# A table of places for the wide halves of a two-layer decoder: the first pair's row block pairs at other distances, its sweep in fewer steps

## The chip, the cores and the metric

The kernel runs on one core of a Trainium2 chip. The time is that of one execution on the device in microseconds (us); the median of three runs of the kernel before is 2098.84 us, the lowest 2098.13 and the highest 2099.01. The engines have short names in the profile: PE is TensorE (PEld its weight loads), DVE is VectorE, ACT is ScalarE, POOL is GpSimd, and SPq is the queue of SyncE, which here issues nearly all DMAs.

## The reference

The kernel computes a trunk of two decoder layers over 256 tokens of width 2048, all in fp32. Layer 0 mixes tokens by attention with a forget gate, layer 1 by a mixture of dilated windows; behind each mixer comes an MLP, and the change lies in the two MLPs alone:

```python
def sq_relu_mlp(h, w_up, w_down):
    a = jax.nn.relu(h @ w_up)
    return (a * a) @ w_down

def reference(x, ...):
    for i in range(DEPTH):
...
        x = x + mix.astype(x.dtype)
        h = rms_norm(x, mlp_norm_g[i])
        x = x + sq_relu_mlp(h, mlp_w_up[i], mlp_w_down[i]).astype(x.dtype)
    return x
```

`w_up` is 2048 x 8192 and `w_down` is 8192 x 2048, so that the weights of one MLP fill 128 MB and each is read once.

## The kernel before

**Products.** Every weight matrix is read in row block pairs: a tile `raw` holds two blocks of 128 rows by 512 columns. ScalarE rounds it to `wh` (fp32r, line L403), VectorE makes the remainder `wl` = raw - wh (L404), and TensorE multiplies the transposed activations by both. Such a triple raw, wh, wl is called a piece here. A plain piece takes 12 matmuls of 128x512 (L452 to L454: two row blocks, two tiles of 128 tokens, three products hi*hi, hi*lo and lo*hi). An output of 512 columns takes 8 plain pieces, and the kernel counts them: a count is one plain piece. Pieces are prepared five ahead of TensorE (`W_BUFS`), and `raw` tiles are loaded five ahead of those (`RAW_BUFS`).

**Wide halves.** Of the 16 outputs of `h @ w_up` in an MLP (4 blocks b of 4 outputs n) ten are made two at a time by a Strassen-Winograd scheme, with seven products where the plain way takes eight. Its two by two are two token tiles and two row blocks on one side, two row blocks and two outputs on the other. One row block pair of such a pair of outputs is a triple of pieces, 6 matmuls each (L1119 to L1121): the "crossed" piece (two `raw` tiles are read for it, `raw` n-1 and n), the "differences" piece, whose source `sd` VectorE makes at L400, and the "sums" piece, whose source `v` VectorE makes at L406 and L407. They go into PSUM tiles named wide_n_tp, wide_n_sc and wide_n_acc. A row block pair costs VectorE three L404, one L400, one L406 and one L407. The last product of the seven is plain row blocks again; one piece of 6 matmuls serves two row block pairs, and these four pieces at a pair's end are called its sweep. Behind a pair's last triple `wide_chain` combines the six PSUM tiles on VectorE (L1083 to L1090), squares on ScalarE, transposes on VectorE (L1037) and sends the result through device memory: sixteen DMAs of 64 KB write it (`held`, L359), four read it back later (`back`).

**Token sums.** The activation side of the scheme needs sums and differences of the transposed activations of each of the 8 row block pairs. `token_sums` makes them during the first pair: four operations on VectorE (L568 to L573, tile `room`), a rounding on ScalarE (L587) and a remainder on VectorE (L591). Its waits are counted in steps of the jobs, and a step is one row block of a plain piece or one piece of a triple.

**What sets the order.** The program is recorded in one order and pinned to it; no scheduler moves anything. `Jobs` runs the side jobs (token sums, chains of finished products) at steps. `wide_slots` says behind which count a piece of a triple stands, and it is read twice: by `add_mlp`, which puts the loads and the preparation into the plan, and by `mlp`, which puts the matmuls there. There are five pairs, in `WIDE`: (1, 0) comes first and is the one that runs beside the token sums; counts 0 to 15 are the first two outputs, 16 to 31 the other two of block 0, 32 to 39 and 40 to 47 the first two outputs of the product with `w_down`.

SyncE's queue issues DMAs strictly in the program's order, each waits on one of eight semaphores that the DMA eight before it used, and a `raw` load waits until its buffer has been read.

Of the kernel before, what the change touches and what calls it, by code (L numbers as in the profile page):

```python
# [23 lines left out]
KC = D // P  # L24
# [22 lines left out]
SUM_TAGS = ("kh3", "kl3", "kh4", "kl4", "kh5", "kl5", "q0", "q1", "q2", "qkw0", "qkw1", "qkw2", "pT", "t1")  # L47

WIDE = ((1, 0), (2, 0), (2, 2), (3, 0), (3, 2))
WIDE_FROM = 15  # L50
UP_ALONE = ((2, 3), (2, 3), (), ())


def wide_slots():

    count = WIDE_FROM
    for b, n in WIDE:
        for pr in range(KC // 2):
            while count % 8 not in (7, 2, 5):
                count += 1  # L60
            yield count, (b, n, 0, pr)
            yield count, (b, n, 1, pr)
            yield count + 1, (b, n, 2, pr)
            count += 2
        count += count % 8 != 7
        for pr in range(0, KC // 2, 2):
            yield count, (b, n, 3, pr)
            count += count % 8 != 7 or pr % 4 == 2
        count += 1


class Jobs:
# [52 lines left out]
def trunk(ctx: ExitStack, tc, x, fox_w_in, fox_b_f, fox_q_gain, fox_k_gain, fox_w_out, dil_w_in,  # L125
# [202 lines left out]
    def add_mlp(l):  # L328
        woven["count"] = 0
        for at, (b, n, what, pr) in wide_slots():  # L330
            woven["due"].setdefault(at, []).append((mlp_w_up[l], b * D + n * NC, what, pr))
        for b in range(4):
            if b == 0:
                add_group(*((mlp_w_up[l], [(n * NC, NC)]) for n in range(2)))
            for n in UP_ALONE[b]:
                add(mlp_w_up[l], (0, D), [(b * D + n * NC, NC)])
            down = mlp_w_down[l][b * D:(b + 1) * D]
            together = 3 if b == 3 else 0
            add_group(*((down, [(n * NC, NC)]) for n in range(together)), parts=LAST_DOWN_PARTS)
            for n in range(together, NX):  # L340
                add(down, (0, D), [(n * NC, NC)])
        woven["due"] = {}
# [785 lines left out]
    def mlp(tag, **after):  # L1128
# [21 lines left out]
        for at, slot in wide_slots():  # L1150
            woven["due"].setdefault(at, []).append(slot)
# [149 lines left out]
```

## Time and profile before

| what | value |
|---|---|
| median of three runs | 2098.84 us |
| the profiled execution's own time | 2096.45 us |
| its span in the profile | 2094.6 us |
| TensorE busy | 2080.3 us, 9835 matmuls |
| VectorE busy | 1730.1 us |
| ScalarE busy | 1294.0 us |
| mean granted TensorE clock | 0.998 |
| loads of 512 KB from `w_up`, issue to landing | median 5.0 us |
| writes of 64 KB (`held`), first MLP and second MLP | median 4.5 and 4.3 us |

Times below are us from the start of the span. In the profile a row of the timeline gives start, duration, engine, line, operation and operands; a number in brackets is the engine's idle time before it, with what ended it. A matmul's record lasts longer than its share, since matmuls overlap: the distance of two starts is what it costs. The tiles' buffer numbers are left out in the profile (`wl`), and stand in the listings of the order (`wl162`, the remainder of piece 162). The first pair of the first MLP begins with piece 144, that of the second MLP with piece 620.

### The profile page before, as it was taken

The numbers are of one execution on the slowest core, as the hardware profiler recorded it, in microseconds if no ns is written. First come the engines' busy times: TensorE is split into PE (matmuls) and PEld (weight loads), VectorE is DVE, ScalarE is ACT, GpSimd is POOL, SyncE is SP. The second block draws the span as 40 slices with busy tenths as digits, with TensorE's granted clock in tenths as the row PEclk, the third lists the DMA queues.
The fourth block names the chain that finished last, engine by engine and source line by source line (L and its number), as shares of the span: only waits on it lengthen the run. The fifth ranks groups of instructions, "written<-read, shape, count | busy, mean of one in ns | idle before, by whom it ended". The sixth has DMA issues, their size and how long they took to land.

```text
span 2094.6 us, 28771 instructions
## 1 busy us (share of the span) xinstructions
PE 2080.3 (99%) x9835; PEld 1825.0 (87%) x9835; DVE 1730.1 (83%) x2215; ACT 1294.0 (62%) x1777; POOL 134.8 (6%) x142
## 2 busy tenths in 40 slices
PE   9999999999999999999999999999999999999999
PEld 7888888878888888888888888888888888888888
DVE  6888876998889889888668787767998899898874
ACT  6565654766666757574656565556666676666662
POOL 2000000000010011010010010000000100110100
PEclk9999999999999999999999999999999999999999
DMA  8888877878898898898877876868878988988985
GB/s 259 253 266 258 261 248 222 256 255 263 272 279 269 266 287 261 275 281 252 282 245 229 249 237 210 264 209 243 265 245 271 277 278 259 275 275 274 276 278 169
DMA packets 385874, 539.02 MB, mean 257 GB/s; under 512 B 43752, under 2 KB 177216, under 8 KB 385728
## 3 DMA queue, kind: packets, MB, share of 16 engines
q1 hardware_dynamic: 371488, 524.21, 78.9%
q0 software_dynamic: 13824, 12.59, 4.0%
q8 instruction: 77, 1.26, 0.3%
q10 hardware_dynamic: 416, 0.39, 0.1%
q14 instruction: 69, 0.57, 0.1%
HBM read 484.09 MB, written 40.39 MB: 250 GB/s over the span
## 4 chain that ended last, share of the span: by engine, by line
PE 87%; DVE 6%; DMA 3%; issue 1%; ACT 1%; SPq 1%; POOL 0%; DVEq 0%; ACTq 0%; POOLq 0%
PE acc L452 23%; PE acc L453 23%; PE acc L454 23%; DVE wl L404 3%; PE wide_n_tp L1120 2%; PE wide_n_tp L1119 2%; PE wide_n_tp L1121 2%; DMA raw<-in_mlp_w_up_dram 2%; PE wide_n_sc L1120 2%; PE wide_n_sc L1121 2%; PE wide_n_sc L1119 1%; PE wide_n_acc L1121 1%; PE wide_n_acc L1119 1%; PE wide_n_acc L1120 1%; ACT wh L403 1%
## 5 line engine op out<-in xcount | busy, mean ns | idle before, releaser
L404 DVE TENSOR_TENSOR wl<-raw,wh 128x1024 fp32r<-128x1024 f32 (+1 forms) x763 | 919.8, 1214 | 305.8 <-ACT wh L403 292.1
L403 ACT CAST wh<-raw 128x1024 fp32r<-128x1024 f32 (+1 forms) x763 | 787.7, 1045 | 531.0 <-PE acc L454 350.3
L452 PE MATMUL acc<-wh,hT_n 128*128 128x512 f32 x1280 | 487.7, 381 | 0.3 <-ACT hT_n L610 0.3
L453 PE MATMUL acc<-wl,hT_n 128*128 128x512 f32 x1280 | 486.8, 380 | 0.3 <-DVE wl L404 0.3
L454 PE MATMUL acc<-wh,hT_n 128*128 128x512 f32 x1280 | 486.3, 380 | 0.0
L454 PEld LDWEIGHTS acc<-wh,hT_n 128*128 128x128 f32 x1280 | 243.0, 190 | 34.2 <-DVE hT_n L611 0.4
L453 PEld LDWEIGHTS acc<-wl,hT_n 128*128 128x128 f32 x1280 | 243.2, 190 | 33.7 <-DVE wl L404 1.6
L452 PEld LDWEIGHTS acc<-wh,hT_n 128*128 128x128 f32 x1280 | 243.2, 190 | 33.0 <-ACT hT_n L610 0.6
L454 PE MATMUL acc<-wh,aTl_n1a 128*128 128x512 f32 x512 | 194.4, 380 | 0.0
L452 PE MATMUL acc<-wh,aTh_n1a 128*128 128x512 f32 x512 | 194.3, 380 | 0.0
L453 PE MATMUL acc<-wl,aTh_n1a 128*128 128x512 f32 x512 | 194.3, 380 | 0.0
L454 PE MATMUL acc<-wh,aTl_n3a 128*128 128x512 f32 x480 | 182.3, 380 | 0.0
L453 PE MATMUL acc<-wl,aTh_n3a 128*128 128x512 f32 x480 | 182.2, 380 | 0.0
L452 PE MATMUL acc<-wh,aTh_n3a 128*128 128x512 f32 x480 | 182.1, 379 | 0.0
L975 POOL DMA_DIRECT2D x<-y_n x96 | 84.2, 1364 | 970.8 <-ACT y_n L974 914.8
L403 ACT CAST wh<-sd 128x1024 fp32r<-128x1024 f32 x80 | 84.0, 1050 | 85.8 <-DVE sd L400 64.4
L403 ACT CAST wh<-v 128x1024 fp32r<-128x1024 f32 x80 | 84.0, 1050 | 50.6 <-PE acc L454 38.9
L454 PEld LDWEIGHTS acc<-wh,aTl_n1a 128*128 128x128 f32 x512 | 97.0, 189 | 13.7 <-DVE aTl_n1a L1069 0.2
L452 PEld LDWEIGHTS acc<-wh,aTh_n1a 128*128 128x128 f32 x512 | 97.0, 190 | 13.4
L453 PEld LDWEIGHTS acc<-wl,aTh_n1a 128*128 128x128 f32 x512 | 97.0, 190 | 13.5
L400 DVE TENSOR_TENSOR sd<-raw,raw 128x1024 f32<-128x1024 f32 x80 | 97.6, 1220 | 8.3 <-DMA raw<-in_mlp_w_up_dram 8.1
L454 PEld LDWEIGHTS acc<-wh,aTl_n3a 128*128 128x128 f32 x480 | 91.0, 190 | 12.8 <-DVE aTl_n3a L1069 0.2
(659 smaller groups left out, 3093.3 us busy)
## 6 DMA issues: line engine op xcount, KB each, us to landing
raw<-in_mlp_w_up_dram SPq DMA_DIRECT2D x296, 512.0 KB, 5.0
raw<-in_mlp_w_down_dram SPq DMA_DIRECT2D x256, 512.0 KB, 5.2
raw<-in_dil_w_in_dram SPq DMA_DIRECT2D x192, 256.0 KB, 3.9
raw<-in_fox_w_in_dram SPq DMA_DIRECT2D x94, 512.0 KB, 5.0
raw<-in_fox_w_out_dram SPq DMA_DIRECT2D x32, 512.0 KB, 4.7
raw<-in_dil_w_in_dram SPq DMA_DIRECT2D x32, 512.0 KB, 5.9
raw<-in_dil_w_out_dram SPq DMA_DIRECT2D x32, 512.0 KB, 4.5
x<-y_n POOLq DMA_DIRECT2D x96, 128.0 KB, 6.4
```

What stands on the lines that cost most here:

```text
L400: nc.vector.tensor_sub(quarters[0], raw, raws[n - 1][:, 1, :].unsqueeze(1).to_broadcast([P, RAW_SUB, NC]))
L403: nc.scalar.copy(hi[:, part, :], raw[:, part, :])
L404: nc.vector.tensor_sub(lo[:, part, :], raw[:, part, :], hi[:, part, :].bitcast(F32))
L452: nc.tensor.matmul(acc[t], ah[:, tok], hi, start=first, stop=False)
L453: nc.tensor.matmul(acc[t], ah[:, tok], lo, start=False, stop=False)
L454: nc.tensor.matmul(acc[t], al[:, tok], hi, start=False, stop=last)
L975: nc.gpsimd.dma_start(xt[n][:, t, h * HC:h * HC + HC], y, accum_op=ALU.add)
L1119: nc.tensor.matmul(banks[bank], ah, wh, start=what < 3 and of == 0, stop=False, **alone)
L1120: nc.tensor.matmul(banks[bank], ah, wl, start=False, stop=False, **alone)
L1121: nc.tensor.matmul(banks[bank], al, wh, start=False, stop=of == KC // 2 - 1, **alone)
```

## The change

The function that computed the places by a rule becomes a table of numbers, one row for each pair: eight places for its row block pairs, then four for its sweep. For four of the five pairs the table holds the numbers that the rule gave. For the first pair they differ: its row block pairs stood behind counts 15, 18, 21, 23, 26, 29, 31, 34 and now stand behind 15, 19, 23, 26, 29, 31, 34, 37; its sweep stood behind 37, 38, 39, 39 and now stands behind 39, 39, 40, 40. The second pair begins behind count 42 in both. The table is used in both MLPs. No instruction is added or removed; lines below the table have numbers five lower.

```diff
--- before.py
+++ after.py
@@ -47,26 +47,21 @@
 SUM_TAGS = ("kh3", "kl3", "kh4", "kl4", "kh5", "kl5", "q0", "q1", "q2", "qkw0", "qkw1", "qkw2", "pT", "t1")
 
 WIDE = ((1, 0), (2, 0), (2, 2), (3, 0), (3, 2))
-WIDE_FROM = 15
+WIDE_AT = ((15, 19, 23, 26, 29, 31, 34, 37, 39, 39, 40, 40), (42, 45, 47, 50, 53, 55, 58, 61, 63, 63, 64, 65),
+           (69, 71, 74, 77, 79, 82, 85, 87, 90, 91, 92, 93), (95, 98, 101, 103, 106, 109, 111, 114, 117, 118, 119, 119),
+           (122, 125, 127, 130, 133, 135, 138, 141, 143, 143, 144, 145))
 UP_ALONE = ((2, 3), (2, 3), (), ())
 
 
 def wide_slots():
 
-    count = WIDE_FROM
-    for b, n in WIDE:
+    for (b, n), at in zip(WIDE, WIDE_AT):
         for pr in range(KC // 2):
-            while count % 8 not in (7, 2, 5):
-                count += 1
-            yield count, (b, n, 0, pr)
-            yield count, (b, n, 1, pr)
-            yield count + 1, (b, n, 2, pr)
-            count += 2
-        count += count % 8 != 7
+            yield at[pr], (b, n, 0, pr)
+            yield at[pr], (b, n, 1, pr)
+            yield at[pr] + 1, (b, n, 2, pr)
         for pr in range(0, KC // 2, 2):
-            yield count, (b, n, 3, pr)
-            count += count % 8 != 7 or pr % 4 == 2
-        count += 1
+            yield at[KC // 2 + pr // 2], (b, n, 3, pr)
 
 
 class Jobs:
```

VectorE in the first MLP, around the first pair's fourth row block pair: twelve rows before the change, up to the "differences" piece of that row block pair (`wl162<-sd`).

```order
L404 TENSOR_TENSOR wl160_4466<-raw157_4355,wh160_4465 128x1024
L1066 TENSOR_TENSOR aTl_n1a0_1_4457<-back_n1a0_1_0_4357,aTh_n1a0_1_4456 128x4x128
L400 TENSOR_TENSOR sd_159_4481<-raw159_4388,raw158_4369 128x1024
L404 TENSOR_TENSOR wl161_4480<-raw159_4388,wh161_4479 128x1024
L406 TENSOR_TENSOR v_159_4482<-raw159_4388,sd_159_4481 128x512
L407 TENSOR_TENSOR v_159_4482<-raw158_4369,v_159_4482 128x512
L568 TENSOR_TENSOR room_n1_3806<-hT_n1_6_4012 128x512
L571 TENSOR_TENSOR room_n1_3806<-room_n1_3806 128x128
L572 TENSOR_TENSOR room_n1_3806<-room_n1_3806 128x128
L573 TENSOR_TENSOR room_n1_3806<-room_n1_3806 128x256
L1069 TENSOR_TENSOR aTl_n1a0_1_4457<-back_n1a0_1_1_4371,aTh_n1a0_1_4456 128x4x128
L404 TENSOR_TENSOR wl162_4504<-sd_159_4481,wh162_4503 128x1024
```

VectorE now, at the same number of pieces:

```order
L399 TENSOR_TENSOR wl159_4449<-sd_157_4430,wh159_4448 128x1024
L1061 TENSOR_TENSOR aTl_n1a0_1_4453<-back_n1a0_1_0_4357,aTh_n1a0_1_4452 128x4x128
L399 TENSOR_TENSOR wl160_4470<-raw158_4377,wh160_4469 128x1024
L1064 TENSOR_TENSOR aTl_n1a0_1_4453<-back_n1a0_1_1_4365,aTh_n1a0_1_4452 128x4x128
L399 TENSOR_TENSOR wl161_4489<-v_157_4431,wh161_4488 128x1024
L563 TENSOR_TENSOR room_n1_3806<-hT_n1_6_4012 128x512
L566 TENSOR_TENSOR room_n1_3806<-room_n1_3806 128x128
L567 TENSOR_TENSOR room_n1_3806<-room_n1_3806 128x128
L568 TENSOR_TENSOR room_n1_3806<-room_n1_3806 128x256
L399 TENSOR_TENSOR wl162_4513<-raw159_4392,wh162_4512 128x1024
L399 TENSOR_TENSOR wl163_4528<-raw160_4410,wh163_4527 128x1024
L586 TENSOR_TENSOR sums_n1_6_1_4519<-room_n1_3806,sums_n1_6_0_4518 128x512
```

Piece 162 belonged to the fourth row block pair; it is a plain piece now, and the fourth row block pair (`sd_162`) begins only behind piece 163; the remainders of the transposed activations (`aTl`) and the token sums (`room`) stand at nearly the same pieces as they did.

SyncE's queue at the second pair's first two row block pairs (`raw191/192` and `raw196/197` serve the first and second, `raw200/201` the third): before.

```order
L359 DMA held_n1a1_1_0_5109<-turned_n1a1_1_0_5108 32x4x128 x4
L378 DMA raw194_5140<-in_mlp_w_down_dram 128x2x512
L359 DMA held_n1a1_1_1_5124<-turned_n1a1_1_1_5123 32x4x128 x4
L378 DMA raw195_5174<-in_mlp_w_down_dram 128x2x512
L378 DMA raw196_5191<-in_mlp_w_up_dram 128x2x512
L378 DMA raw197_5193<-in_mlp_w_up_dram 128x2x512
L378 DMA raw198_5229<-in_mlp_w_down_dram 128x2x512
L359 DMA held_n1a1_0_0_5232<-turned_n1a1_0_0_5231 32x4x128 x4
L359 DMA held_n1a1_0_1_5241<-turned_n1a1_0_1_5240 32x4x128 x4
L378 DMA raw199_5277<-in_mlp_w_down_dram 128x2x512
L378 DMA raw200_5293<-in_mlp_w_up_dram 128x2x512
L378 DMA raw201_5310<-in_mlp_w_up_dram 128x2x512
```

And now:

```order
L373 DMA raw194_5144<-in_mlp_w_down_dram 128x2x512
L373 DMA raw195_5156<-in_mlp_w_down_dram 128x2x512
L373 DMA raw196_5185<-in_mlp_w_up_dram 128x2x512
L373 DMA raw197_5187<-in_mlp_w_up_dram 128x2x512
L354 DMA held_n1a1_1_0_5190<-turned_n1a1_1_0_5189 32x4x128 x4
L373 DMA raw198_5221<-in_mlp_w_down_dram 128x2x512
L354 DMA held_n1a1_1_1_5203<-turned_n1a1_1_1_5202 32x4x128 x4
L354 DMA held_n1a1_0_0_5248<-turned_n1a1_0_0_5247 32x4x128 x4
L373 DMA raw199_5273<-in_mlp_w_down_dram 128x2x512
L354 DMA held_n1a1_0_1_5257<-turned_n1a1_0_1_5256 32x4x128 x4
L373 DMA raw200_5293<-in_mlp_w_up_dram 128x2x512
L373 DMA raw201_5310<-in_mlp_w_up_dram 128x2x512
```

The sixteen writes of the first pair's results (`held`, x4 is four rows that are alike) stand closer together: four of them came ahead of `raw194`, and now all sixteen stand between `raw197` and `raw200`, with `raw198` and `raw199` among them.

ScalarE at the end of the third output of block 0 (`acc146` is its PSUM tile, which the next output, n = 3, uses again): before.

```order
L403 CAST wh162_4503<-sd_159_4481 128x1024
L587 CAST sums_n1_6_0_4513<-room_n1_3806 128x512
L403 CAST wh163_4522<-raw160_4390 128x1024
L403 CAST wh164_4535<-v_159_4482 128x1024
L1014 ACTIVATE a_n1a0_2_0_4551<-acc146_0_4263 128x512
L1014 ACTIVATE a_n1a0_2_1_4552<-acc146_1_4264 128x512
```

And now:

```order
L1057 CAST aTh_n1a0_1_4452<-back_n1a0_1_0_4357 128x4x128
L1057 CAST aTh_n1a0_1_4452<-back_n1a0_1_1_4365 128x4x128
L398 CAST wh160_4469<-raw158_4377 128x1024
L398 CAST wh161_4488<-v_157_4431 128x1024
L1009 ACTIVATE a_n1a0_2_0_4508<-acc146_0_4256 128x512
L1009 ACTIVATE a_n1a0_2_1_4509<-acc146_1_4257 128x512
```

The two activations that free that PSUM tile stand behind the casts of pieces 160 and 161 now, and ahead of them two casts that need a read back from device memory (`back_n1a0_1`).

## The prediction

> **What bounds the kernel now.** I read the page first, then the list of waits, then TensorE's timeline at its longest waits and VectorE's at the same places.
>
> ```profile
> span 2094.6 us, 28771 instructions
> PE wide_n_sc L1120 <- DVE wl L404: 7.7, 5, 2.5
> ```
>
> TensorE bounds the kernel, and nearly all its waiting once it is under way is one wait: the second piece of a row block pair, for VectorE's remainder. The change moves exactly such pieces. TensorE's timeline there (first MLP, then second, then the second pair's start):
>
> ```profile
> 406.40 0.38 PE L1119 MATMUL wide_n_tp<-wh,hT_n 128*128 128x512 f32 x1
> 411.36 0.38 PE L454 MATMUL acc<-wh,hT_n 128*128 128x512 f32 x1
> 412.42 0.38 PE L1120 MATMUL wide_n_acc<-wl,sums_n 128*128 128x512 f32 x1
> 431.63 0.38 PE L1119 MATMUL wide_n_sc<-wh,sums_n 128*128 128x512 f32 x1
> 433.13 0.48 PE L1120 MATMUL wide_n_sc<-wl,sums_n 128*128 128x512 f32 x1 [1.12 <-DVE wl L404]
> 442.53 0.38 PE L1119 MATMUL wide_n_sc<-wh,sums_n 128*128 128x512 f32 x1
> 445.40 0.79 PE L1120 MATMUL wide_n_sc<-wl,sums_n 128*128 128x512 f32 x1 [2.49 <-DVE wl L404]
> 447.27 0.63 PE L1121 MATMUL wide_n_sc<-wh,sums_n 128*128 128x512 f32 x1
> 447.69 0.63 PE L452 MATMUL acc<-wh,hT_n 128*128 128x512 f32 x1
> 448.79 0.38 PE L452 MATMUL acc<-wh,hT_n 128*128 128x512 f32 x1
> 1488.78 0.38 PE L1119 MATMUL wide_n_tp<-wh,hT_n 128*128 128x512 f32 x1
> 1513.39 0.38 PE L1119 MATMUL wide_n_sc<-wh,sums_n 128*128 128x512 f32 x1
> 1531.08 0.38 PE L453 MATMUL acc<-wl,hT_n 128*128 128x512 f32 x1
> 540.19 0.38 PE L1119 MATMUL wide_n_tp<-wh,hT_n 128*128 128x512 f32 x1
> 544.41 0.38 PE L452 MATMUL acc<-wh,aTh_n1a 128*128 128x512 f32 x1
> ```
>
> The first two rows are 23 matmuls apart: 4.96 / 23 = 0.2157 us each. Every other stretch is held against that. From 411.36 to 412.42 are 2 steps, so 0.63 is lost (this one waits for ScalarE). From 431.63 to 442.53 are 42 steps (9.06): 1.84 lost. From 442.53 to 448.79 are 9: 4.32 lost, of which the wait is 2.65 and the rest is matmuls 0.43 apart (447.27 to 447.69), at half speed. First MLP: 6.79. Second: 1513.39 to 1531.08 are 55 steps (11.86), 5.83 lost. The second pair's start, first MLP alone: 12 steps (2.59) in 4.22, 1.63 lost. Together 14.25 us.
>
> Why VectorE is late shows in the stretches (columns: busy time of PE, PEld, DVE, ACT, POOL, granted clock, DMA share, GB/s):
>
> ```profile
> 400.00:425.00 25.00, 24.64 (x115) 21.31 (x114) 24.73 (x33) 17.34 (x24) 0.00 (x0) 1.00 0.74 222
> 425.00:450.00 25.00, 21.21 (x89) 17.41 (x88) 24.73 (x32) 15.21 (x21) 0.00 (x0) 0.93 0.75 241
> 450.00:475.00 25.00, 25.00 (x118) 21.95 (x117) 24.83 (x31) 14.76 (x19) 0.00 (x0) 1.00 0.82 260
> 475.00:500.00 25.00, 25.00 (x118) 21.95 (x117) 22.56 (x24) 16.85 (x20) 0.00 (x0) 1.00 0.82 257
> ```
>
> VectorE is busy 24.73 of 25 us while the token sums are made: it is the bound in this stage, and only there. The clock falls to 0.93 in the stretch with the 2.65 us wait.
>
> **The change, worked out.** No instruction is added, so the question is where VectorE's work falls against TensorE's. VectorE's timeline gives the price of each operation as the distance to the next start:
>
> ```profile
> 400.92 1.22 DVE L404 TENSOR_TENSOR wl<-raw,wh 128x1024 fp32r<-128x1024 f32 x1
> 420.75 1.30 DVE L1037 STREAM_TRANSPOSE turned_n1a<-a_n1a 128x512 f32<-128x512 f32 x2
> 421.97 1.18 DVE L404 TENSOR_TENSOR wl<-v,wh 128x1024 fp32r<-128x1024 f32 x1
> 423.07 0.68 DVE L591 TENSOR_TENSOR sums_n<-room_n,sums_n 128x512 fp32r<-128x512 f32 x1
> 423.67 2.35 DVE L404 TENSOR_TENSOR wl<-raw,wh 128x1024 fp32r<-128x1024 f32 x2
> 425.94 1.22 DVE L400 TENSOR_TENSOR sd<-raw,raw 128x1024 f32<-128x1024 f32 x1
> 427.08 1.22 DVE L404 TENSOR_TENSOR wl<-raw,wh 128x1024 fp32r<-128x1024 f32 x1
> 428.21 0.69 DVE L406 TENSOR_TENSOR v<-raw,sd 128x512 f32<-128x512 f32 x1
> 429.54 0.69 DVE L568 TENSOR_TENSOR room_n<-hT_n 128x512 f32<-128x512 f32 x1
> 431.26 0.68 DVE L1066 TENSOR_TENSOR aTl_n1a<-back_n1a,aTh_n1a 128x512 fp32r<-128x512 f32 x1
> 431.86 1.22 DVE L404 TENSOR_TENSOR wl<-sd,wh 128x1024 fp32r<-128x1024 f32 x1
> 444.12 1.22 DVE L404 TENSOR_TENSOR wl<-sd,wh 128x1024 fp32r<-128x1024 f32 x1
> 1482.23 1.22 DVE L404 TENSOR_TENSOR wl<-raw,wh 128x1024 fp32r<-128x1024 f32 x1
> ```
>
> A remainder or an `sd` costs 1.135, the two operations on `v` 1.33 (428.21 to 429.54), the four on `room` 1.72, a rest of token sums 0.60, a transpose 0.61 to 0.63, an `aTl` 0.60. A triple thus takes VectorE 4 x 1.135 + 1.33 = 5.87 us while TensorE spends 18 x 0.2157 = 3.88 on it; a plain piece takes 1.135 against 2.59. Fewer triples early is what VectorE needs.
>
> *Test on the order before.* From 400.92 to the fourth row block pair's second piece (162): 18 remainders and 3 `sd` (23.8), 4 `v` (5.3), 4 `room` (6.9), 4 sums (2.4), 4 transposes (2.5), 4 `aTl` (2.4): 43.3, plus the last remainder's own 1.22, gives 445.5; the trace ends it at 445.34. TensorE, 157 matmuls after 406.40 and with the 0.63, would want it at 440.89: 4.6 short, which is what the two waits take (1.84 + 2.65).
>
> *The order now.* I made the same sum at every piece up to 176. The largest shortage is at the sixth row block pair's second piece (176), with 289 matmuls ahead of it: 32 remainders and 5 `sd` (42.0), 6 `v` (8.0), 5 `room` (8.6), 6 rests of sums (3.7), 6 transposes (3.7), 6 `aTl` (3.6): 69.6, so VectorE ends at 400.92 + 69.6 + 1.22 = 471.74, against 406.40 + 62.34 + 0.63 = 469.37. Shortage 2.37, with 0.06 from its end to the matmul 2.43. It grows in steps of 0.7 or less (pieces 160 to 176), none near 2.65, so I take no half speed. First MLP: 0.63 + 2.43 = 3.06 instead of 6.79, gain 3.73. The second MLP begins with more lead (VectorE at 1482.23, TensorE at 1488.78) and without the 0.63: 1482.23 + 70.82 + 0.06 - 1488.78 - 62.34 = 1.99 instead of 5.83, gain 3.84. Sum 7.57.
>
> *What that takes for granted: that VectorE never waits.* The new order on ScalarE puts two casts of read-back data and that of `raw158` ahead of piece 160's remainder.
>
> ```profile
> 435.14 0.62 ACT L1062 CAST aTh_n1a<-back_n1a 128x512 fp32r<-128x512 f32 x1 [0.73 <-DMA back_n1a<-held_n1a]
> ```
>
> That is when the same read landed before. Piece 160's remainder is due at 437.2 by the same sum (16 remainders, 2 `sd`, 3 `v`, 3 `room`, 4 sums, 4 transposes, 3 `aTl` behind 400.92), so there are 2 us of room, less the two casts. Bounds: 0 and 2 us of idling in each MLP; I take 0.3, nearest to the row, which still has room. The activations that free the PSUM tile of the third output stand behind piece 161's cast, whose `v` VectorE ends about 434.6; should TensorE wait a little for them, it waits earlier for what VectorE's shortage costs it anyway: bounds 0 and 0.8, taken as 0.
>
> *The second pair's start.* Here the queue's order changes.
>
> ```profile
> 516.36 0.69 DVE L407 TENSOR_TENSOR v<-raw,v 128x512 f32<-128x512 f32 x1
> 519.65 0.96 SPq L378 DMA_DIRECT2D raw<-in_mlp_w_up_dram  x2
> 522.12 6.99 SPq L359 DMA_DIRECT2D held_n1a<-turned_n1a  x8
> 529.70 2.16 SPq L378 DMA_DIRECT2D raw<-in_mlp_w_up_dram  x2
> 538.35 1.23 DVE L400 TENSOR_TENSOR sd<-raw,raw 128x1024 f32<-128x1024 f32 x1 [2.51 <-DMA raw<-in_mlp_w_up_dram]
> ```
>
> Before, the buffers for `raw196/197` are read by 517.05, but the queue issues them only at 519.65, behind writes; eight more writes take to 529.11, `raw200/201` go out up to 531.86 and land 6.49 later, and TensorE loses 1.63. Now everything up to the second pair is 3.73 earlier: the buffers are read about 513.3 and `raw196/197` go out ahead of all sixteen writes. Behind them stand sixteen writes and two loads. At 6.99 / 8 = 0.87 a write and 0.48 a load `raw200/201` are out by 514.3 + 13.9 + 1.9 = 530.1 and land at 536.6; at 0.48 for all, only the reading of their buffers holds them (12 us after `raw196/197` as before, about 526), landing at 532.5. The third row block pair begins on TensorE at 540.19 - 3.73 = 536.5, so its `sd` has to start by 534.3 (1.135 for it, 1.22 for the remainder, less one matmul). So the loss lies between 0 and 3.5 in each MLP: 2.3 at the first piece and up to 1.2 at the second, where 1.33 of `v` comes ahead. It was 1.63 and 0. I take 0.3 in each, since the early end is nearer to the rows: what made the loads late before, a load pair that was late itself, is gone. 1.63 - 0.6 = 1.0 gained.
>
> The sum: 7.6 - 0.6 + 1.0 = 8.0 us. Against the profiled execution, 2096.45 (its span 2094.6 and 1.85 around it), 2088.4; the median before is 2.39 above that execution, so 2098.84 - 8.0 = **2090.8 us**.
>
> [...]
>
> **Rivals.**
> - *The slow clock has another cause and stays.* As the mechanism of this kernel: a spell of 4.32 - 2.65 = 1.67 comes back in each MLP wherever the stage runs. Gain 8.0 - 3.3 = 4.7, 2094.1. Against it: waits of 1.12 and less are followed by full speed. 5%.
> - *VectorE idles for casts and loads and the shortage stays near 5 us, without the slow clock.* Then only about 1.6 is gained: 2097.2. For it: the queue's new order around `back_n1a0_1` and `raw158`. Against it: 2 us of room. 11%.
> - *The writes hold `raw200/201` until a wait like that at 445.40 comes back, once in each MLP.* It costs 4.32 twice: 7.57 + 1.63 - 8.64 = 0.6 gained, 2098.3. It decides once the loads land 2.4 late, after 536.7; the worst landing above is 536.6. 10%.
> - *Slower: that wait at two row block pairs of the second pair in both MLPs*, since a late load there frees its buffers late and the next pair's loads go out late as well (as `raw196/197` did to `raw200/201` above). 4 x 4.32 = 17.3 against 9.2: 2106.9. It needs landings after 536.7 that the next row block pair does not make up. 9%.
>
> **How the numbers follow.** The forecast has 65%; its own range is 2088.2 (everything gained: 9.2, with 1.4 for run to run and rounding) to 2093.5 (2 us of idling or 1.6 of late loads in both). A measurement here tells a change from none at about 0.2%, 4.2 us. Faster by more: forecast and slow clock, 70%; within: idling and one late load, 21%; slower: 9%. The range for 8 in 10 reaches from 2088.2 to 2098.5.
>
> **What would show it.** Right: the waits of wide_n_sc for VectorE in the first pair are each below 1 us and sum to about 4; granted clock 1.00 in the stretches of 25 us around 445 and 1527 alike; VectorE still above 24.5 of 25 us there. Wrong: a wait of 2 us or more with slow matmuls behind it, at the first pair or between pieces 205 and 216; VectorE waiting for ScalarE's casts between 430 and 480; `raw200/201` issued later than 530.

## The result, and the profile after

The changed kernel takes 2091.68 us (median; 2089.37 to 2094.50) where the kernel before takes 2099.16 us (2098.13 to 2099.76). The ratio is 0.9966, 95% interval 0.9956 to 0.9976: 7.5 us faster, 5 to 9 by the interval. The forecast was 2090.8 us.

The profiled execution of the changed kernel is its longest one, 2094.50 us, 2.8 above the median, while that of the kernel before was 2.7 below its median. The two profiles alone differ by 1.8 us in span. So the stages are compared here one by one, and traces of kernels that share a stage's places stand beside them. First the span and three rows of TensorE's list of waits in the changed kernel (total, times, longest); the kernel before had 7.7 us in five waits in its first row. (The count of instructions is eight lower than before: eight fewer instructions that only wait for a semaphore were recorded. The working instructions are the same in number.)

```profile
span 2092.8 us, 28763 instructions
PE wide_n_sc L1115 <- DVE wl L399: 1.8, 2, 0.9
PE wide_n_acc L1114 <- ACT a_n1a L1009: 1.7, 1, 1.7
PE acc L448 <- DVE wl L399: 1.7, 6, 0.4
```

The long waits for VectorE are gone, but TensorE now waits for it several times, 0.91 us at most. In TensorE's timeline (first MLP, then second, then the first MLP's last products with `w_down`):

```profile
415.60 0.48 PE L1114 MATMUL wide_n_acc<-wh,sums_n 128*128 128x512 f32 x1 [1.71 <-ACT a_n1a L1009]
446.43 0.48 PE L448 MATMUL acc<-wl,hT_n 128*128 128x512 f32 x1 [0.43 <-DVE wl L399]
454.07 0.48 PE L1115 MATMUL wide_n_sc<-wl,sums_n 128*128 128x512 f32 x1 [0.91 <-DVE wl L399]
460.46 0.48 PE L448 MATMUL acc<-wl,hT_n 128*128 128x512 f32 x1 [0.26 <-DVE wl L399]
1494.41 0.48 PE L1114 MATMUL wide_n_acc<-wh,sums_n 128*128 128x512 f32 x1 [0.44 <-ACT a_n3a L1009]
1525.23 0.48 PE L448 MATMUL acc<-wl,hT_n 128*128 128x512 f32 x1 [0.43 <-DVE wl L399]
1532.88 0.48 PE L1115 MATMUL wide_n_sc<-wl,sums_n 128*128 128x512 f32 x1 [0.91 <-DVE wl L399]
959.62 0.48 PE L449 MATMUL acc<-wh,aTl_n1a 128*128 128x512 f32 x1 [0.28 <-DVE aTl_n1a L1064]
```

The stretches correspond to those shown of before (PE, PEld, VectorE, ScalarE, GpSimd, granted clock, DMA share, GB/s); the last is the second pair's start, where 1.63 us was lost:

```profile
400.00:425.00 25.00, 23.29 (x109) 20.08 (x108) 24.59 (x38) 16.07 (x23) 1.07 (x1) 1.00 0.79 229
425.00:450.00 25.00, 24.57 (x114) 21.02 (x113) 24.26 (x32) 16.01 (x22) 0.00 (x0) 1.00 0.80 256
450.00:475.00 25.00, 23.68 (x106) 19.36 (x105) 24.20 (x30) 14.49 (x17) 0.00 (x0) 1.00 0.78 251
536.00:546.00 10.00, 10.00 (x48) 8.74 (x48) 9.77 (x10) 8.46 (x11) 3.52 (x4) 1.00 0.79 246
```

The clock stays at 1.00, VectorE is still the busy engine of the stage but no longer quite full (24.73 before), and the second pair starts without a loss. With every distance of two matmul starts held against 0.2157 us (the forecast's column has its 0.3 of idling in each MLP added to the shortage):

| loss in us | before | forecast | after, this execution |
|---|---|---|---|
| first MLP, for ScalarE at the first sums piece | 0.63 | 0.63 | 1.98 |
| first MLP, for VectorE, with the slow clock | 6.16 | 2.73 | 3.5 |
| second MLP, for ScalarE at the first sums piece | 0 | 0 | 0.71 |
| second MLP, for VectorE, with the slow clock | 5.83 | 2.29 | 3.53 |
| second pair's start, both MLPs | 1.63 | 0.6 | 0 |
| last products with `w_down` of the first MLP, near 958 | 0 | 0 | 0.66 |
| sum | 14.25 | 6.25 | 10.4 |

By these two traces the places gain 3.9 us, not the 7.5 of the medians. The two spans differ by less still, 1.8 us, since this execution is 2.1 us late before the change can act: its first triple begins at 408.54, that of the kernel before at 406.40. Nearly all of that arises in the first 12 us, where its matmuls stand 0.43 us apart until the full clock comes, at 11.13 us and at 4.86 in the trace of before.

### The profile page after: what moved, and what is told of

It is laid out like the page before. It is cut to its first block, busy times and chain, and to the rows that moved or that the text cites. A ratio compares the mean times of both kernels' runs of the same rounds, so it can differ in the third digit from the quotient of the medians.

```text
span 2092.8 us, 28763 instructions
## 1 busy us (share of the span) xinstructions
PE 2081.4 (99%) x9835; PEld 1820.4 (87%) x9835; DVE 1729.7 (83%) x2215; ACT 1293.2 (62%) x1777; POOL 134.8 (6%) x142
## 4 chain that ended last, share of the span: by engine, by line
PE 92%; DVE 3%; DMA 2%; ACT 1%; issue 1%; SPq 0%; ACTq 0%; DVEq 0%
PE acc L448 24%; PE acc L447 24%; PE acc L449 24%; PE wide_n_tp L1115 2%; PE wide_n_tp L1114 2%; PE wide_n_tp L1116 2%; PE wide_n_acc L1114 2%; PE wide_n_sc L1115 2%; PE wide_n_acc L1116 2%; PE wide_n_acc L1115 2%; PE wide_n_sc L1114 2%; PE wide_n_sc L1116 2%; DVE wl L399 1%; ACT wh L398 1%; DMA raw<-in_mlp_w_down_dram 1%
## 5 line engine op out<-in xcount | busy, mean ns | idle before, releaser
L399 DVE TENSOR_TENSOR wl<-v,wh 128x1024 fp32r<-128x1024 f32 x80 | 97.4, 1218 | 7.8 <-ACT wh L398 7.1
```

What stands on the lines that cost most here:

```text
L399: nc.vector.tensor_sub(lo[:, part, :], raw[:, part, :], hi[:, part, :].bitcast(F32))
```

## The experiments

**The sweep alone.** The row block pairs stand as before, the sweep as changed.

```diff
-WIDE_AT = ((15, 19, 23, 26, 29, 31, 34, 37, 39, 39, 40, 40), ...
+WIDE_AT = ((15, 18, 21, 23, 26, 29, 31, 34, 39, 39, 40, 40), ...
```

> The row block pairs of the first pair stand as before (15, 18, 21, 23, 26, 29, 31, 34); only its sweep is closed up (39, 39, 40, 40). Theory (VectorE runs short while token sums are made, so where the row block pairs stand is what counts): the waits of the first pair stay as in the kernel before, 6.8 us lost in the first MLP and 5.8 in the second, each with a spell of half clock; only the 1.6 us at the second pair's start may go. 2097.5 to 2099.2 us. Rival (it is the sweep, or what moves behind it, that gained): 2091.7 us, and the waits above 2 us gone.

2100.94 us, ratio to the kernel before 1.0015 (1.0006 to 1.0024): slower by a little, and above the 2097.5 to 2099.2 expected. From its list of waits:

```profile
PE wide_n_sc L1115 <- DVE wl L399: 7.2, 4, 2.5
PE acc L449 <- DVE aTl_n1a L1064: 1.4, 2, 1.1
PE acc L449 <- DVE aTl_n3a L1064: 1.1, 1, 1.1
```

The waits of the first pair stay, with the slow clock (6.3 us and 6.2 lost for VectorE). The loss at the second pair's start is gone. New are two losses of 1.3 us where the product with `w_down` takes up activations that were read back (505.87 in the first MLP): VectorE makes the remainder `aTl` in the same order as before, between operations that combine the first pair, and TensorE, with two pieces of the sweep fewer ahead of that place, arrives sooner. The rival falls; by itself this half of the change costs.

**The row block pairs alone**, with a sweep that is as open as before behind them.

```diff
-WIDE_AT = ((15, 19, 23, 26, 29, 31, 34, 37, 39, 39, 40, 40), ...
+WIDE_AT = ((15, 19, 23, 26, 29, 31, 34, 37, 39, 40, 41, 41), ...
```

> The row block pairs as in the changed kernel, and its sweep one step of places later and more open (39, 40, 41, 41, as wide as before; no smaller places are free behind the last pair). Theory (the row block pairs carry the gain): 2091.7 us as the changed kernel, 3.5 us lost for VectorE in each MLP, and within 1.6 us of it for what this does at the second pair's start. Rival (the closed up sweep carries it): 2097 us or more.

2093.64 us, ratio 0.9976 (0.9965 to 0.9987). It lies 2 us above the changed kernel, a difference that the two intervals (0.9965 to 0.9987, 0.9956 to 0.9976) do not establish. In the first pair the same 3.5 us are lost for VectorE; at the second pair's start two waits come (519.01 and 1599.55, 0.64 and 1.16 us lost), and 1.7 us are lost near 957. So the row block pairs carry most of the gain, 5.1 of 7.5 us by the medians. That the closed up sweep serves to leave room ahead of the second pair is what the two waits suggest; the times do not show it.

**The first MLP alone.** `wide_slots` gives the new row for the first MLP and the old one for the second (the line is shortened: `NEW` and `OLD` stand for the two rows).

```diff
+    for (b, n), at in zip(WIDE, ((OLD if second else NEW,) + WIDE_AT[1:])):
```

> The new places in the first MLP only; the second MLP keeps those of before. Theory (two separate stages, each with its own shortage): the first MLP's share of what the traces show recovered is about two thirds (6.79 + 1.63 - 4.13 = 4.3 us of 6.6), so about 4.9 of the 7.5 us gained: 2094.3 us, with 5.8 us lost and a spell of half clock in the second MLP alone. Rival (what is gained in the first MLP is given back or doubled by a shift of the later stages): outside 2092.5 to 2096.

2094.23 us, ratio 0.9981 (0.9971 to 0.9990), as expected. The first MLP loses 4.0 us here (0.48 for ScalarE, 3.53 for VectorE), the second 6.4, 0.8 of it for ScalarE. The old wait is there; the second row is a wait that the kernel before does not have, and the third is the same old wait in the run with the sweep alone:

```profile
1524.27 0.48 PE L1115 MATMUL wide_n_sc<-wl,sums_n 128*128 128x512 f32 x1 [2.49 <-DVE wl L399]
1538.18 0.48 PE L448 MATMUL acc<-wl,hT_n 128*128 128x512 f32 x1 [0.17 <-DVE wl L399]
1530.09 0.79 PE L1115 MATMUL wide_n_sc<-wl,sums_n 128*128 128x512 f32 x1 [2.49 <-DVE wl L399]
```

One thing differs from the expectation: no slow clock follows this wait. The matmuls behind 1524.27 start 0.22 us apart, those behind 1530.09 in the other run 0.43. Yet the second MLP loses 5.5 us for VectorE here and 6.2 there, 0.7 more and not 1.67: without the slow clock 0.7 us is lost at 1536.45 and 1538.18, where the other run loses nothing. Both begin with the same lead of VectorE (6.1 us, counted below), and the row block pairs stand at the same places. The last two sections come back to it.

**Less work for VectorE, in the old order.** Three of the four operations on `room` are left out of the kernel before, so that its token sums, and with them its output, are not the reference's.

```diff
-            a12, a22, a11, a21 = (to[:, i, :] for i in range(4))
-            nc.vector.tensor_add(a21, a21, a22)
-            nc.vector.tensor_sub(a11, a11, a21)
-            nc.vector.tensor_add(to[:, 0:2, :], to[:, 0:2, :], a11.unsqueeze(1).to_broadcast([P, 2, P]))
```

> The kernel before, with three of the four operations on room left out of each token sum (the output is then not the reference's): 0.33 + 0.33 + 0.34 = 1.0 us of VectorE less, eight times in each MLP, and nothing else moved to another engine. Theory (VectorE's amount of work is the bound): by the fourth row block pair VectorE has 4 us less behind it, so the shortage of 4.6 us falls below 1; no wait of 2 us, no half clock: 5.7 us gained in the first MLP, 5.4 in the second, 2087 to 2089 us. Rival (loads or ScalarE's order set those waits): no change, 2097 us or more.

2084.32 us, ratio 0.9937 (0.9922 to 0.9952): 14.4 us gained, more than the 11 expected. In the stretches of the first pair:

```profile
400.00:425.00 25.00, 25.00 (x117) 21.91 (x116) 24.93 (x30) 18.87 (x25) 0.00 (x0) 1.00 0.86 268
425.00:450.00 25.00, 24.87 (x114) 21.18 (x113) 24.90 (x30) 16.26 (x20) 0.00 (x0) 1.00 0.81 260
450.00:475.00 25.00, 25.00 (x117) 21.89 (x117) 24.93 (x28) 17.36 (x21) 0.00 (x0) 1.00 0.87 274
```

With 1.0 us less per token sum TensorE does not stop, at the old places and with the same loads; only 0.6 us is lost in the first MLP's first pair, 0.1 in the second's, and at the second pair's start 0.2. VectorE's amount of work caused these losses: some 13 of the 14.25 us listed above are gone in the trace. The medians give 14.4 us, with an interval of 10 to 16. A shorter `room` also lets ScalarE's cast of the sums begin sooner; but in the kernel before VectorE idles only 0.27 us in each stretch of 25 from 400 to 450, so that waiting for such casts can hold no more than 0.5 of the 6.16 us lost.

**The same work on GpSimd.** All four operations on `room`, in the kernel before, moved from `nc.vector` to `nc.gpsimd`.

> The kernel before, with the four operations on room of each token sum (1.72 us of VectorE, eight times in each MLP) done by GpSimd, which is idle there. Theory (VectorE's amount of work is the bound): VectorE gets 13.8 us back in each MLP, no wait of wide_n_sc for a remainder above 0.5 us and no half clock are left with the old places, 12 us gained: about 2087 us. Rival (loads or ScalarE set those waits, or GpSimd's work slows VectorE's or comes too late): 2095 us or more, waits of 1 us and more left.

2116.45 us, ratio 1.0091 (1.0076 to 1.0106): slower by 18. The group of the first of the four operations, then ScalarE's and VectorE's timelines:

```profile
L568 POOL TENSOR_TENSOR room_n<-hT_n 128x512 f32<-128x512 f32 x16 | 38.4, 2399 | 282.8 <-DVE hT_n L555 201.6 <-ACT wh L403 40.1 <-DVE sums_n L591 33.8
416.04 0.62 ACT L587 CAST sums_n<-room_n 128x512 fp32r<-128x512 f32 x1 [4.24 <-POOL room_n L573]
411.19 2.30 DVE L404 TENSOR_TENSOR wl<-raw,wh 128x1024 fp32r<-128x1024 f32 x1
```

The operation takes 2.4 us where VectorE took 0.7; VectorE's remainder in the third row, beside GpSimd's work, takes 2.30 us in place of 1.22; and ScalarE's cast of the sums, which stands in ScalarE's order ahead of three casts and the activations that free a PSUM tile, waits 4.24 us, so that TensorE waits 4.0 at 420.04. The operation was replaced by a slower one in the same place in every queue, and the run says nothing on VectorE's amount of work. Of the 39 remainders that run beside GpSimd's four operations, 15 take 1.22 us as ever, 10 take 1.47 and 14 take 1.75 to 2.31.

**Further apart.**

```diff
-WIDE_AT = ((15, 19, 23, 26, 29, 31, 34, 37, 39, 39, 40, 40), ...
+WIDE_AT = ((15, 21, 26, 29, 31, 33, 35, 37, 39, 39, 40, 40), ...
```

> Row block pairs of the first pair at 15, 21, 26, 29, 31, 33, 35, 37, sweep as in the changed kernel: the second to fourth stand further apart still, the last four closer. Theory (VectorE's sum of work): the sum for the second MLP gives a shortage of 0 where the changed kernel's gives 1.99 (it measured 3.5, about 1.1 of it VectorE idling for casts); 4.8 to 7 us less than the changed kernel, 2084.7 to 2087 us. Rival (loads or the reads that bring the outputs back can't follow, or the last four pairs become the short place): 2091 us or more.

2093.74 us, ratio 0.9980 (0.9971 to 0.9990). Not one wait for VectorE's remainder is left in the first pair, as the sum of VectorE's work had it, and yet nothing is gained over the changed kernel where 4.8 to 7 us were expected. TensorE's timeline and ScalarE's:

```profile
440.06 0.48 PE L447 MATMUL acc<-wh,hT_n 128*128 128x512 f32 x1 [3.09 <-ACT a_n1a L1009]
438.47 1.05 ACT L398 CAST wh<-raw 128x1024 fp32r<-128x1024 f32 x1 [1.88 <-DMA raw<-in_mlp_w_up_dram]
439.42 1.08 ACT L1009 ACTIVATE a_n1a<-acc 128x512 f32<-128x512 f32 x2
```

The fourth output's first matmul needs the PSUM tile of the third, which two activations free. They stand in ScalarE's order behind the cast of the piece five ahead, and with a pair at 26 that is the cast of a crossed piece, whose two loads land only at 438.4. TensorE stands still 3.25 us there and 2.63 in the second MLP. This is the wait that the forecast named for the PSUM tile of the third output and put at 0: right for the changed kernel, wrong for this spread. In this execution no slow clock follows; nine of the ten have a mean granted clock of 0.998 or 0.999, where this one has 1.000.

**ScalarE's casts of the token sums one step later.**

```diff
-            yield 2
+            yield 3
             if pr < KC // 2 - 1:
```

> The changed kernel, with ScalarE's cast and VectorE's rest of each token sum one step of the planner later. Theory (in the changed kernel 1.1 us of the 3.5 lost in each MLP is VectorE idling at two casts of plain pieces that stand behind a cast of token sums): the two idle times go, 2.4 us lost in each, 2.2 us gained: 2089.5 us. Rival (the idle time only moves to another cast, or was covered): 2091.7 us, 3.5 us lost as before.

The idle time it aims at, in the changed kernel's timelines of VectorE and ScalarE:

```profile
446.87 1.23 DVE L399 TENSOR_TENSOR wl<-raw,wh 128x1024 fp32r<-128x1024 f32 x1 [0.50 <-ACT wh L398]
459.19 1.23 DVE L399 TENSOR_TENSOR wl<-raw,wh 128x1024 fp32r<-128x1024 f32 x1 [0.59 <-ACT wh L398]
445.27 0.62 ACT L582 CAST sums_n<-room_n 128x512 fp32r<-128x512 f32 x1 [3.42 <-DVE room_n L568]
445.80 1.04 ACT L398 CAST wh<-raw 128x1024 fp32r<-128x1024 f32 x1
```

ScalarE waits for `room`, and the next piece's cast, though its data are there, waits behind; VectorE, which made `room`, then has nothing to do for 0.5 us.

2091.98 us, ratio 0.9967 (0.9954 to 0.9980), the time of the changed kernel. In the trace both idle times are gone in the second MLP, where 2.4 us are lost for VectorE instead of 3.5; in the first MLP another one came (0.86 us at 431.38), and 3.6 are lost, with 0.4 more for ScalarE at 441.22. What the second MLP shows, 1.1 us, is below what the times can tell apart.

**The activations first.** The second output's two activations go into ScalarE's queue ahead of the casts of the pieces that follow (the diff is shortened to its main lines).

```diff
-                steps(banks[n], range(a, b))
-                if b == KC:
+                steps(banks[n], range(a, b), *((post,) if early and b == KC else ()))
+                if b == KC and not early:
                     jobs.spawn(post(banks[n]))
```

> The changed kernel, with the two activations that free the PSUM tile of the second output put into ScalarE's queue before the casts of the pieces that follow, not behind them. Theory (the wait at the first row block pair's sums piece is for ScalarE's order): 415.6's wait goes, 0.6 to 2.0 us in the first MLP and up to 0.7 in the second; about 2090.0 us, with the waits for VectorE kept at 3.5 us and shifted. Rival (what is gained there is lost again at VectorE's waits behind it, since VectorE is short by then and gains no work): no change, 2091.7 us.

2097.10 us, ratio 0.9995 (0.9986 to 1.0005): 5.4 us slower than the changed kernel, outside both expectations. The waits at the first sums piece are gone in both MLPs. In the first MLP two others stand in their place, and VectorE's timeline has the reason:

```profile
425.77 0.48 PE L1115 MATMUL wide_n_sc<-wl,sums_n 128*128 128x512 f32 x1 [1.82 <-DVE wl L399]
428.62 0.48 PE L448 MATMUL acc<-wl,hT_n 128*128 128x512 f32 x1 [1.29 <-DVE wl L399]
423.89 0.71 DVE L1032 STREAM_TRANSPOSE turned_n1a<-a_n1a 128x512 f32<-128x512 f32 x1 [1.68 <-DMA held_n1a<-turned_n1a]
```

What follows the activations came earlier with them. The transpose now stands ahead of a remainder that TensorE needs, and waits for a DMA to have read the tile it writes into; VectorE stands still 1.68 us. In the changed kernel the same transpose stood at 424.25, behind that remainder, and did not wait.

**A combination:** row block pairs at 15, 20, 24, 29, 31, 33, 35, 37 and the activations first.

> Row block pairs of the first pair at 15, 20, 24, 29, 31, 33, 35, 37 (sweep as changed) and the activations first as in the run before this one. Theory: VectorE's sum of work leaves no shortage (0 by the same sum that gives 1.99 for the changed kernel), a pair at 24 puts fewer loads ahead of the cast that held the activations in the spread at 15, 21, 26, and the wait at the first sums piece is gone: 7 + 1.3 us less than the changed kernel, 2082.5 to 2085 us. Rival (the fourth output's first matmul waits for the activations as it did there, 2.6 to 3.3 us in each): 2088 to 2090 us.

2110.58 us, ratio 1.0060 (1.0043 to 1.0076), a miss on the wrong side of the kernel before. TensorE's timeline of the first MLP:

```profile
426.13 0.48 PE L1115 MATMUL wide_n_tp<-wl,hT_n 128*128 128x512 f32 x1 [1.88 <-DVE wl L399]
430.31 0.48 PE L1115 MATMUL wide_n_sc<-wl,sums_n 128*128 128x512 f32 x1 [2.62 <-DVE wl L399]
445.04 0.48 PE L447 MATMUL acc<-wh,hT_n 128*128 128x512 f32 x1 [3.18 <-ACT a_n1a L1009]
```

The waits of the last run and the wait of the spread at 15, 21, 26 came together, and the slow clock behind the last. The sum of VectorE's work, which gave 0 for it, knows neither.

**The later pairs alone further apart.** The first three stay.

```diff
-WIDE_AT = ((15, 19, 23, 26, 29, 31, 34, 37, 39, 39, 40, 40), ...
+WIDE_AT = ((15, 19, 23, 28, 31, 33, 35, 37, 39, 39, 40, 40), ...
```

> The changed kernel, with the fourth to seventh row block pair moved back by two, two, two and one (15, 19, 23, 28, 31, 33, 35, 37); the first three and the sweep as changed, so that what ScalarE has ahead of the third output's activations stays as it is. Theory (VectorE's sum of work): the shortage by the sum is 0.5 us in each MLP where the changed kernel's was 2.0 (measured 3.5); with the idle time at casts no larger than there, 1.5 to 3 us gained in each: 2086 to 2089 us. Rival (the room gained is lost to a late load, or to reads and activations, as at 15, 21, 26): 2091 us or more.

2091.47 us, ratio 0.9961 (0.9946 to 0.9975). The loss for VectorE falls to 2.1 us in each MLP, 1.4 less than in the changed kernel, with the third output's tile free in time. The median does not follow: near 957 this trace loses 1.5 us, and 0.6 more at 1576.75, in the second MLP's product with `w_down`.

**Both small edits**, the later pairs and the casts.

> Both edits that took waits away for themselves without moving the time: the fourth to seventh pair later (15, 19, 23, 28, 31, 33, 35, 37) and the casts and rests of the token sums one step of the planner later. Theory (VectorE's idling at the casts is what is left of the shortage): 0.5 to 1 us lost for VectorE in each MLP instead of 1.9, 1.5 to 2.5 us less than the run with the pairs alone: 2089 to 2090 us. Rival (TensorE, ahead of its earlier time, waits at the start of the last down projections near 958 us for data that come no earlier, and gives it back there): 2091 to 2092 us.

2090.34 us, ratio 0.9956 (0.9942 to 0.9970). Between the expectations of 2089 to 2090 and 2091 to 2092; its interval covers most of that of the changed kernel's ratio, so that it is not shown to be better. In the trace 1.2 and 1.6 us are left for VectorE in the first pair, and TensorE waits elsewhere:

```profile
957.18 0.48 PE L449 MATMUL acc<-wh,aTl_n1a 128*128 128x512 f32 x1 [0.98 <-DVE aTl_n1a L1061]
958.38 0.48 PE L449 MATMUL acc<-wh,aTl_n1a 128*128 128x512 f32 x1 [0.29 <-DVE aTl_n1a L1064]
```

These lose 1.8 us with what is smaller around them, and two more of 0.9 each stand where the product with `w_down` takes up the fourth output's activations (498.58 and 1576.77), for remainders that stand behind the making of those activations on VectorE. That is 3.6 us, and what VectorE gains early is partly waited off there. Why the data of the first two waits do not come earlier by as much as TensorE does is not settled: the last two reads of activations before 958 were issued from 949.8 in the changed kernel and in the kernel before, though TensorE was 0.8 us further in the first; in the run with less work on VectorE, 6 to 7 us ahead of both, they went out from 942.8 and nothing was lost.

**Waits made on purpose.** VectorE's remainder of ten pieces is repeated in the changed kernel (shortened: the table `HELD_UP` and a loop of shorter repeats are not shown).

```diff
+        whole, short = HELD_UP.get(i, (0, 0))
+        for _ in range(whole):
+            nc.vector.tensor_sub(lo[:, part, :], raw[:, part, :], hi[:, part, :].bitcast(F32))
```

> The changed kernel, with VectorE's remainder of ten pieces repeated 8 to 10 times (into the same place, so the output stays) where TensorE is 8.07 us behind VectorE: waits of about 1.4 (piece 108), 1.7 (547), 2.2 (439 and 590), 2.5 (118 and 515), 2.9 (465 and 598), 3.3 (580) and 3.7 us (911), 24.9 us in all. Theory (the half clock is decided by windows of 3.41 us that run on from the kernel's start, and comes for the window behind one in which TensorE stood still for more than a share between 2.09 and 2.23 us): no wait below 2.1 gives it, those above give it only where one window holds that much; equal waits may differ. Rival (the length of the wait decides): the same verdict for equal waits, and all above some length give it.

2188.19 us in a single execution, and the waits came out otherwise than planned, from 1.3 to 10.5 us: VectorE also does other work that TensorE needs in those stages, and that stood behind the repeated operations. Waits of equal length could not be compared. The windows can still be read, below; there the two bounds are 2.12 and 2.28 us.

## Why the prediction was right, and where not

**What bounds the stage: right.** VectorE's amount of work is the cause, and nothing else had to be touched to remove the losses (the light token sums: some 13 of 14.25 us in the trace).

**The slow clock: it went as forecast, for another reason than the one given, and it was worth less.** All six executions of the changed kernel have a mean granted clock of 1.000. The forecast took the spell of half clock to come from the length of the wait: half clock behind 2.65 us, full speed behind 1.12 us and less. In the run with the first MLP alone the same wait of 2.65 us stands in the second MLP with no spell behind it, so the length does not decide; in the trace that the forecast was read from, both waits fell where they bring a spell, and that was luck. Nor does removing a spell save its 1.67 us: the two runs above differ by 0.7 us, as VectorE seems to catch up while TensorE runs slowly. The clocks of the kernel before say the same. Of 59 executions, 22 have a mean clock of 0.998, like the traces with two spells, and 10 have 1.000, like the traces without any, at the old places; these 10 take 1.4 us less on average. The first rival (slow clock stays, 3.3 us) fell, and its price was more than twice too high.

**VectorE's shortage: the mechanism was right and the term too small.** With the 0.3 of idling, 2.73 and 2.29 us were forecast, 3.5 and 3.53 measured, and 3.5 again in the other traces with these places. The step that failed is *that VectorE never waits*, put at 0.3: it idles 1.1 us in each MLP, which the second MLP of the run with later casts gives back. The place was wrong as well: not the read-back casts and `raw158` (piece 160's cast was done at 439.01 and its remainder began at 440.57), but two casts of plain pieces behind the casts of token sums, whose data VectorE itself had just made. In the second MLP the 1.99 also counted on a lead of VectorE that was not there: 6.55 us from its remainder at 1482.23 to the first triple at 1488.78. In the changed kernel that is 5.39 (1483.23 to 1488.62), and 6.10 with the 0.71 that TensorE then waits for ScalarE; in the first MLP 4.11 and 1.98 give 6.09, as 5.47 and 0.63 gave 6.10 before. With 6.1 the forecast's own sum is 2.43 in both MLPs, and 2.43 + 1.1 is the 3.5 measured.

Of the signs that the forecast named, the waits of wide_n_sc are below 1 us (0.91), but sum to 1.8 in place of about 4, since half of the waiting came at plain pieces (1.7 us). The clock is 1.00. VectorE is busy 24.26 and 24.20 of 25 us there, not above 24.5, and it does wait for ScalarE's casts between 430 and 480: by that sign of being wrong, too, the idling was the step that failed.

**The second pair's start: 0.6 us forecast, 0 measured.** The order in the queue was as expected: sixteen writes went out between the two load pairs. The times agree by accident. `raw196/197` went out from 517.57, not 513.3, the writes took 0.52 us each, near the lower of the two figures (0.48 and 0.87), and `raw200/201` were issued from 529.21 to 530.13 (530.1 expected). They landed at 534.6 and 535.9, within the two ends of 532.5 and 536.6. But TensorE began the third row block pair at 540.99 and not at 536.5: 2.1 us of that is the later start of this execution, 1.35 ScalarE at the first sums piece, 1.1 the idling. `sd` was begun 2.9 us before it had to be. Where less is lost ahead, TensorE's lateness is not needed: in the runs with the later pairs, and with both small edits, the third pair begins at 538.5 and 538.6, `sd` is still 2.3 and 1.6 us early, and nothing is lost.

**A bound of the range.** 2 us of idling in each MLP, in place of the 0.3 taken, would give 2094.2 us and not the 2093.5 named for it; 1.6 of late loads gives 2093.4.

**Not forecast:** 0.71 us for ScalarE at the first sums piece in the second MLP, and 0.66 near 958. At the first sums piece of the first MLP 0.63 was carried over from the one trace, where the kernels with the same first places show 0.5 to 2.0; it varies from execution to execution, and what VectorE has as lead varies with it.

**The sum.** The terms gave 8.0 and the medians 7.5, but the terms do not match one by one. With the 4.0 us of the first MLP in the run with that MLP alone, the 3.7 of the second in the run with the row block pairs alone, and the 0.66, the places lose about 8.4 us, 5.9 less than the trace of before. The other 1.6 us between that and the medians are not located. Some may lie in the trace of before, which lost 12.6 us in its two first pairs where the run with the sweep alone, at the same row block pairs, lost 13.1; executions of the changed kernel differ by 5.1 us from the shortest to the longest. So 8.0 against 7.5 us is in part luck: the shortage was forecast 2.0 us too low in all, ScalarE's 0.7 and the 0.7 near 958 were not in the sum, and 0.6 was allowed at the second pair's start that was not lost.

## What to carry to other kernels

When an engine that feeds TensorE is short for a stretch, a running sum of its work against TensorE's, taken at every piece, is a first guess of where waits come and how far pieces must be moved apart (here 2.43 of the 3.5 us measured in each MLP); add to it the places where that engine's next operation stands behind another engine's wait for its own result (here the other 1.1 us). Once the first shortage was gone here, the next limits were waits inside in-order queues, activations behind a cast that waits for a load (TensorE stood still 3.25 us) or a transpose that waits for a write (VectorE 1.68 us), so move few things at a time and look at the timeline after each. Cutting the short engine's work (1.0 us per token sum, with three operations left out, so a bound and no usable version) gained 14.4 us; the best order that was tried gained 8.4.

## What the runs showed of the hardware

**In these traces half clock came by fixed windows of 3.41 us, not by the length of a wait.** In the trace of before the spells of half clock begin at 445.18 and 1527.21, 317 times 3.4133 us apart, and last 3.41 each. The clock's rise at the start (4.864) and its fall behind the last products (2093.82) lie in the same steps, 129 ahead of the first spell and 166 behind the start of the second; in the changed kernel's trace rise and fall (11.134 and 2093.26) are 610 such steps apart. Cutting a trace at such steps from its own spells (or from the clock's rise at the start) gives windows. Six pairs and one triple of them follow: from the kernel before, the run with the first MLP alone, the run with the activations first, the spread at 15, 21, 26 (the triple), the combination, and the waits made on purpose (two). The columns are as above. In these rows half clock (0.50) goes with how long TensorE stood still in the row ahead:

```profile
441.77:445.18 3.41, 1.14 (x6) 0.65 (x4) 3.31 (x7) 1.54 (x3) 0.00 (x0) 1.00 0.80 267
445.18:448.60 3.42, 3.20 (x8) 2.55 (x9) 3.42 (x5) 3.42 (x6) 0.00 (x0) 0.50 0.39 69
```

```profile
1520.30:1523.71 3.41, 1.48 (x7) 0.95 (x6) 3.31 (x7) 1.20 (x2) 0.00 (x0) 1.00 0.69 216
1523.71:1527.12 3.41, 2.85 (x12) 2.25 (x13) 3.41 (x5) 3.41 (x6) 0.00 (x0) 1.00 0.44 119
```

```profile
424.51:427.92 3.41, 1.56 (x6) 1.05 (x6) 3.31 (x7) 0.46 (x1) 0.00 (x0) 1.00 1.00 321
427.92:431.33 3.41, 2.71 (x13) 2.40 (x14) 3.41 (x4) 3.41 (x5) 0.00 (x0) 1.00 0.87 283
```

```profile
435.10:438.51 3.41, 1.87 (x9) 1.31 (x7) 3.21 (x5) 1.53 (x3) 0.00 (x0) 1.00 1.04 400
438.51:441.92 3.41, 1.86 (x9) 1.65 (x10) 3.38 (x4) 2.92 (x4) 0.00 (x0) 1.00 0.86 311
441.92:445.33 3.41, 3.41 (x17) 3.00 (x16) 3.31 (x7) 1.43 (x3) 0.00 (x0) 1.00 0.75 202
```

```profile
442.77:446.18 3.41, 1.14 (x5) 1.03 (x6) 3.38 (x5) 3.41 (x5) 0.00 (x0) 1.00 0.49 127
446.18:449.60 3.42, 3.42 (x9) 2.72 (x9) 3.32 (x6) 0.95 (x3) 0.00 (x0) 0.50 0.99 357
```

```profile
318.30:321.71 3.41, 1.56 (x6) 0.89 (x6) 3.28 (x9) 1.54 (x3) 0.00 (x0) 1.00 0.88 225
321.71:325.12 3.41, 0.00 (x0) 0.00 (x0) 2.88 (x6) 2.87 (x6) 0.00 (x0) 0.50 0.82 230
1021.45:1024.86 3.41, 1.18 (x5) 1.05 (x6) 3.38 (x5) 0.00 (x0) 0.00 (x0) 1.00 0.04 5
1024.86:1028.27 3.41, 3.41 (x10) 2.69 (x9) 3.41 (x4) 0.00 (x0) 0.00 (x0) 0.50 0.94 294
```

By the distances of starts, a window at full clock in which TensorE stood still up to 2.12 us (424.51, the activations first) was followed by full clock, and one with 2.28 us or more (2.28 at 318.30, the waits made on purpose) by half clock; none of the rows lies between the two. In the two traces of before and after, taken whole from 20 us to the last products, the windows with full clock behind them hold 1.80 us or less, and the two with half clock behind them 2.44 and 2.76. The wait of 3.25 us in the spread lies across two windows (1.70 and 1.55) in this execution and costs no clock; the wait of 2.65 in the kernel before had 2.44 in one and halved it; the same wait with 2.09 in one did not.

**Beside work on GpSimd VectorE was slower:** of the 39 remainders that ran beside GpSimd's operations on `room`, 24 took 1.47 to 2.31 us in place of 1.22.
